# Latent attention: the rotary half of the queries is multiplied out once, its second copy laid by transfers

## The chip, the cores and the metric

The kernel runs on one core of one Trainium2 chip. The metric is the device time of one execution in microseconds (us). A core has TensorE (PE in the profile; its weight loads are the row PEld), VectorE (DVE), ScalarE (ACT), GpSimd (POOL) and SyncE (SP), which here only issues transfers. Each engine works through its own instructions in order and waits at one whose input or buffer is not ready.

## The reference, cut to what matters

Two layers over 256 tokens of width 1024, each with two SwiGLU halves around a token mixer, and a gated embedding behind. The change is in the mixer of the first layer, latent attention with eight heads. A query has 128 plain components and 64 rotary ones; keys and values come from one narrow projection.

```python
c = u @ w_down
c_q, c_kv, k_rope = jnp.split(c, [MLA_Q_LORA, MLA_Q_LORA + MLA_KV_LORA], axis=-1)
q = (rms_norm(c_q, q_norm) @ w_uq).reshape(b, s, MLA_HEADS, MLA_NOPE + MLA_ROPE)
q_nope, q_rope = jnp.split(q, [MLA_NOPE], axis=-1)
q_rope = apply_rope(q_rope, cos[:, :, None, :], sin[:, :, None, :])
k_rope = apply_rope(k_rope, cos, sin)
kv = (rms_norm(c_kv, kv_norm) @ w_ukv).reshape(b, s, MLA_HEADS, MLA_NOPE + MLA_V)
k_nope, v = jnp.split(kv, [MLA_NOPE], axis=-1)
sc = (jnp.einsum('bqhd,bkhd->bhqk', q_nope[:, q0:q1], k_nope[:, :q1])
      + jnp.einsum('bqhr,bkr->bhqk', q_rope[:, q0:q1], k_rope[:, :q1]))
```

The rotation takes the two halves x1, x2 of the 64 components to x1 cos - x2 sin and x2 cos + x1 sin. Scores are masked by chunks of 64 tokens, and softmax and the product with the values follow.

## The kernel before, in words

Activations lie transposed: 128 features on the partitions, 256 tokens along the row. Weights arrive in blocks of 128 x 1024 float32 (`raw`, four buffers). ScalarE rounds a block to a high part (`whi`, line 98), VectorE subtracts to get the low part (`wlo`, line 102: "weight split"), and a product is three: high by high, low by high, high by low (`mm3`, lines 221 to 223). Where both parts of the activations lie side by side, the first and third go as one of 512 columns (lines 236 and 237). `W.pump()` records, at its place in the program, one block's split on VectorE, ScalarE's rounding of up to two blocks ahead, and the fetch of a block four further on; blocks are used in the order of a list, `plan`.

The order on every engine is the order in which the program is written. In `mla` it is: the narrow projection (`pq`, `pkv`, `pr`), its row scale `rb`, the scaled projections and their squares; then `queries(hp, half)` for head pair hp: half 0 are the plain components of two heads (12 products of 256 columns), half 1 the rotary ones (12 products). For the rotation the weight holds the 64 components and, in another 64 columns, the same with their halves swapped. The table `ck` holds the cosine on the first 64 partitions and the signed sine on the other 64, and one multiplication of the 128 rows by `ck` gives what, summed over all 128 partitions against a doubled key (`kr`, made with the matrix `twice`), is the rotated score.

Behind the queries of pair 0 come the keys of all heads (`pk`, 24 products), the values of the first four heads (`values(0, 0)`, `values(1, 0)`), and the row scales: `by_token` (a product `pst`, VectorE's `v`, GpSimd's power `rtok`) and `by_column` (product `pb`, copied by ScalarE to `rb`). `pst` and `pb` share one PSUM buffer. `kT` is `pk` times `rb`, four multiplications on VectorE.

`attention` then runs eleven steps, h = 0 to 10. In step h TensorE does, in this order: fill work, the transposes of head h-3's probabilities (`turn`, `pt`), `project(h, 0)`, the scores of head h-1 (`psc`), `project(h, 1)`, fill work, the value product of head h-3 (`po`). Between them, the maxima `m` and the normalisation of the probabilities `pr` are on VectorE; the exponentials, the copy `ptS` of the transposed probabilities and the copy `os` of a head's result on ScalarE. `project` holds the queries of the pairs to come, and the values of the last four heads (`psv`). Fill work is parts of the output projection over heads that are done, counted per step in `MLA_FILLS` as (step, place): parts. It is done for the first four of eight output blocks; the rest of the products follow behind the last step.

Of the kernel before, what the change touches and what calls it, by code (L numbers as in the profile page):

```python
# [11 lines left out]
F32 = mybir.dt.float32  # L12
# [3 lines left out]
AF = mybir.ActivationFunctionType  # L16
ALU = mybir.AluOpType
AX = mybir.AxisListType

P = 128  # L20
D = 1024
T = 256
# [3 lines left out]
H = 8  # L26
# [3 lines left out]
ROPE = 64  # L30
# [10 lines left out]
GAINS = 80  # L41


MLA_FILLS = {(7, 1): 2, (8, 0): 4, (8, 1): 4, (9, 0): 4, (9, 1): 4, (10, 0): 3, (10, 1): 3}
FOX_FILLS = {(8, 0): 4, (8, 1): 7, (9, 0): 6, (9, 1): 5}

PI_IN = 3.1415925
# [94 lines left out]
def trunk(ctx, tc, xT, xt, pT, pos, freq, bf, ffn_first, ffn_in, ffn_out, w_down, w_uq, w_ukv, mla_o,  # L142
          fox_qk, fox_v, fox_f, fox_o, ple_gate, ple_proj, ple_rows, gain_row, out):
    nc = tc.nc
    const = ctx.enter_context(tc.tile_pool(name="const", bufs=1))
# [3 lines left out]
    work = ctx.enter_context(tc.tile_pool(name="work", bufs=2))  # L149
# [4 lines left out]
    plan = []  # L154
# [11 lines left out]

    plan_ffn(0)
    plan.extend(w_down[c] for c in range(4))
    plan.append(w_uq[0])
    plan.extend(w_ukv[c] for c in range(2))  # L170
    plan.extend(w_uq[c] for c in range(1, H // 2))
    plan.extend(mla_o[d] for d in range(KD))
    plan_ffn(1)
    plan_ple()
# [31 lines left out]
    def bank(name, shape=(P, 2, T)):  # L206
        return psum.tile(list(shape), F32, name=name, tag="mm")

    W = Weights(nc, wp, plan)
# [347 lines left out]
    def mla(norm, nxt):  # L557
# [25 lines left out]
        block(pr, norm.pair)  # L583
        turned = tmp("turned")
        nc.vector.tensor_mul(turned, pr, cr)
        kr = work.tile([P, T], F32, name="kr", bufs=1)
        W.pump()

        kq, v = keys_values()
        kT, qT, qr = kq[:, :8, :], kq[:, 8:16, :], kq[:, 16:24, :]  # L590
        held = []

        def queries(hp, half):
            if half == 0:
                held[:] = W.get()
            ps = bank("ps")
            for s in range(2):
                part(ps[:, s, :], held[0], nq.pair, range(2), at=lambda k: k * 512 + (2 * half + s) * P)
            if half == 0:
                nc.scalar.activation(qT[:, 2 * hp:2 * hp + 2, :], ps, AF.Copy)  # L600
            else:
                W.done(held[0])
                nc.vector.tensor_mul(qr[:, 2 * hp:2 * hp + 2, :], ps,
                                     ck.rearrange("p (o t) -> p o t", o=1).to_broadcast([P, 2, T]))

        queries(0, 0)
        queries(0, 1)
        nkv.by_token()
        W.pump()
        pk = bank("pk", (P, T))  # L610
        nc.tensor.matmul(pk, twice, turned, start=True, stop=True)
        nc.scalar.activation(kr, pk, AF.Copy)
        w, = W.get()
        pk = []
        for hp in range(H // 2):
# [2 lines left out]
                part(ps[:, s, :], w, nkv.pair, range(1), at=lambda k: (2 * hp + s) * P)  # L618
            pk.append(ps)
        W.done(w)  # L620
        w, = W.get()

        def values(t, c):

            ps = bank("psv", (P, 512))
            mm3(ps, [nkv.pair[:, 0, a, t * P:(t + 1) * P] for a in range(2)],
                [a[:, c * 512:(c + 1) * 512] for a in w[1:]], True, True)
            if t == c == 0:
                nkv.by_column()
                for i in range(H // 2):  # L630
                    nc.vector.tensor_mul(kT[:, 2 * i:2 * i + 2, :], pk[i], nkv.rb2)
            nc.scalar.activation(v[:, t, c * 512:(c + 1) * 512], ps, AF.Copy, scale=nkv.rtok[:, t:t + 1])

        values(0, 0)
        nq.by_token()
        W.pump()
        values(1, 0)

        qscale = work.tile([P, 2], F32, name="qscale", bufs=1)
# [1 line left out]
        W.pump()  # L641

        def project(h, half):
            if half == 0 and h < H - 2:
                queries(h // 2 + 1, h % 2)
            elif half and h % 2:
                W.pump()

            if (h, half) == (H - 2, 1):
                values(0, 1)  # L650
            elif (h, half) == (H - 1, 0):
                values(1, 1)
                W.done(w)

        def score(h, dst, diagonal):
            for t in range(2):
                nc.tensor.matmul(dst[t], qT[:, h, t * P:(t + 1) * P], kT[:, h, :(t + 1) * P], start=t == 0, stop=False)
            masked(diagonal, 0)
            for t in range(2):
                nc.tensor.matmul(dst[t], qr[:, h, t * P:(t + 1) * P], kr[:, :(t + 1) * P], start=False, stop=t == 1)  # L660

        attention(project, score, v, qscale, nxt, 3, MLA_FILLS, 4)

# [253 lines left out]
    a = 0  # L917
# [48 lines left out]
    fr = const.tile([P, 1], F32, name="fr")  # L966
    cs = const.tile([P, 2, T], F32, name="cs")
    ck = const.tile([P, T], F32, name="ck")
    twice = const.tile([P, P], F32, name="twice")

    def tables():
        nc.gpsimd.memset(bf_sb, 0.0)
# [93 lines left out]
        for i, a in enumerate(half):  # L1066
            nc.vector.tensor_copy(ck[a, :], cs[a, i, :])
            yield
            for b in half:
                nc.vector.tensor_copy(twice[a, b], ident[a, a])  # L1070
                yield

    n1 = Norm(G_MIX, KD, D)
    ffn(n0, n1, None, first, tables())
# [17 lines left out]
def _cols(w, n):  # L1092

    k, m = w.shape
    return np.ascontiguousarray(w.reshape(k // P, P, m // n, n).transpose(2, 1, 0, 3)).reshape(m // n, P, -1)


def _layout(x, p, positions, ffn_norm, ffn_w_in, ffn_w_out, mix_norm, mla_w_down, mla_q_norm, mla_w_uq,
# [28 lines left out]
    a["w_down"] = _cols(np.concatenate([cq, ckv, kr, ks], axis=1), P)  # L1127

    w = mla_w_uq[0].reshape(256, H // 2, 2, 192)
    nope, rope = w[..., :128], w[..., 128:]  # L1130
    swap = np.concatenate([rope[..., 32:], rope[..., :32]], axis=-1)
    rope = np.concatenate([rope, swap], axis=-1)
    w = np.concatenate([b.reshape(256, H // 2, -1) for b in (nope, rope)], axis=-1)
    a["w_uq"] = _cols(w.reshape(256, -1), 512)
    w = mla_w_ukv[0].reshape(P, H, 2, P)
    a["w_ukv"] = np.ascontiguousarray(w.transpose(2, 0, 1, 3)).reshape(2, P, D)
    a["mla_o"] = _cols(mla_w_o[0], P)
# [42 lines left out]
```

## Time and profile before

| | before |
|---|---|
| median of 3 runs | 1001.46 us (1001.19 to 1002.36) |
| profiled execution, own time | 1001.46 us |
| its span, first to last instruction | 999.7 us |
| granted TensorE clock, mean | 0.998 |
| busy: PE, DVE, ACT, POOL | 988.8, 740.5, 517.6, 423.7 us |
| latent attention, first product to first product of the next stage | 192.00 to 267.12 us of the span |

Timeline rows read: start and duration in us, engine, line, operation, output<-input, shape, count, and in brackets how long the engine stood idle before it and what ended that. TensorE's products overlap: the time that one takes in a stream is the distance between two starts, not its printed duration. Rows of groups end in count, busy time and mean duration.

### The profile page before, as it was taken

How to read it: one execution, taken by the hardware profiler on the slowest of the kernel's cores; microseconds unless marked ns; L12 is line 12 of the kernel's file. 1: busy time of each engine (PE TensorE's matmuls, PEld its weight loads, DVE VectorE, ACT ScalarE, POOL GpSimd, SP SyncE). 2: the span in 40 equal slices, each digit the busy share in tenths (PEclk: the TensorE clock that was granted, in tenths of full speed). 3: DMA queues.
4: the chain of work that ended last, by engine and by line, in shares of the span. 5: the costliest groups of instructions: out<-in, count | busy, mean ns of one | idle time of the engine just before them, and what ended most of it. 6: DMA issues, size and time to landing. Idle time of an engine off the chain costs nothing.

```text
span 999.7 us, 16018 instructions
## 1 busy us (share of the span) xinstructions
PE 988.8 (99%) x5940; PEld 875.1 (88%) x5940; DVE 740.5 (74%) x1051; ACT 517.6 (52%) x825; POOL 423.7 (42%) x348
## 2 busy tenths in 40 slices
PE   9999999999999999999999999999999999999996
PEld 7888888998988888889888888899889888888886
DVE  5777879676768787667778876666777778876674
ACT  7555444456655544555555444546445554544552
POOL 0777730110267775111477673211221577671120
PEclk9999999999999999999999999999999999999999
DMA  8566666651456666665366656666443566666561
GB/s 330 177 209 208 190 181 191 187 169 53 132 182 207 189 190 185 193 196 195 127 198 206 192 182 192 180 194 206 151 142 102 189 202 199 189 179 201 178 210 43
DMA packets 51388, 180.54 MB, mean 181 GB/s; under 512 B 5872, under 2 KB 6000, under 8 KB 51312
## 3 DMA queue, kind: packets, MB, share of 16 engines
q1 hardware_dynamic: 50880, 178.75, 57.3%
q8 instruction: 47, 0.77, 0.3%
q10 hardware_dynamic: 432, 0.79, 0.3%
q14 instruction: 29, 0.24, 0.1%
HBM read 178.46 MB, written 1.05 MB: 180 GB/s over the span
## 4 chain that ended last, share of the span: by engine, by line
PE 91%; DVE 4%; ACT 2%; issue 1%; POOL 0%; DMA 0%; POOLq 0%; SPq 0%; ACTq 0%; DVEq 0%
PE pu L236 16%; PE po L236 16%; PE pg L236 16%; PE po L237 8%; PE pu L237 8%; PE pg L237 8%; PE ps L236 4%; PE ps L237 2%; DVE wlo L102 1%; PE ps L221 1%; PE ps L223 1%; PE ps L222 1%; PE pv L221 1%; PE pv L223 1%; PE pv L222 1%
## 5 line engine op out<-in xcount | busy, mean ns | idle before, releaser
L102 DVE TENSOR_TENSOR wlo<-raw,whi 128x1024 fp32r<-128x1024 f32 (+2 forms) x338 | 416.8, 1241 | 17.8 <-ACT whi L98 17.1
L98 ACT ACTIVATE whi<-raw 128x1024 fp32r<-128x1024 f32 (+2 forms) x338 | 336.4, 1027 | 20.9 <-DMA raw<-in_ffn_in_dram 12.9
L331 POOL TENSOR_TENSOR gu<-two 128x256 f32<-128x256 f32 x176 | 235.5, 1339 | 117.9 <-DVE two L329 108.4
L236 PE MATMUL pg<-u,whi 128*128 128x512 f32 x704 | 251.7, 395 | 0.8 <-ACT whi L98 0.4
L236 PE MATMUL pu<-u,whi 128*128 128x512 f32 x704 | 251.1, 395 | 0.0
L236 PE MATMUL po<-hs,whi 128*128 128x512 f32 x704 | 246.0, 394 | 0.0
L237 PE MATMUL pg<-u,wlo 128*128 128x256 f32 x704 | 198.2, 282 | 0.3 <-DVE wlo L102 0.2
L237 PE MATMUL po<-hs,wlo 128*128 128x256 f32 x704 | 198.1, 281 | 0.0
L237 PE MATMUL pu<-u,wlo 128*128 128x256 f32 x704 | 198.0, 281 | 0.0
L236 PEld LDWEIGHTS pg<-u,whi 128*128 128x128 f32 x704 | 132.2, 188 | 32.1 <-DVE u L280 1.3
L236 PEld LDWEIGHTS pu<-u,whi 128*128 128x128 f32 x704 | 132.2, 188 | 30.3
L236 PEld LDWEIGHTS po<-hs,whi 128*128 128x128 f32 x704 | 132.2, 188 | 30.2
L237 PEld LDWEIGHTS pg<-u,wlo 128*128 128x128 f32 x704 | 132.5, 188 | 0.9 <-DVE wlo L102 0.9
L237 PEld LDWEIGHTS pu<-u,wlo 128*128 128x128 f32 x704 | 132.5, 188 | 0.0
L237 PEld LDWEIGHTS po<-hs,wlo 128*128 128x128 f32 x704 | 132.5, 188 | 0.0
L291 POOL TENSOR_TENSOR acc<-acc,sq 128x256 f32<-128x256 f32 x42 | 46.0, 1094 | 173.7 <-ACT sq L286 173.5
L213 ACT ACTIVATE hs<-hid 128x256 fp32r<-128x256 f32 x88 | 36.8, 418 | 142.1 <-POOL hid L349 140.1
L349 POOL TENSOR_TENSOR hid<-sg,gu 128x256 f32<-128x256 f32 x88 | 105.2, 1196 | 7.0 <-POOL gu L331 0.2
L217 DVE TENSOR_TENSOR hs<-hid,hs 128x256 fp32r<-128x256 f32 x88 | 63.5, 721 | 48.6 <-ACT hs L213 48.6
L329 DVE TENSOR_TENSOR two<-pg,rb 128x512 f32<-128x512 f32 x88 | 60.3, 685 | 46.8 <-PE pg L237 38.9
L275 ACT ACTIVATE u<-state 128x256 fp32r<-128x256 f32 x57 | 29.0, 509 | 125.7 <-DVE state L392 104.3
L343 ACT ACTIVATE sg<-gu 128x256 f32<-128x256 f32 x88 | 36.8, 418 | 78.5 <-POOL gu L331 78.5
(247 smaller groups left out, 1189.2 us busy)
## 6 DMA issues: line engine op xcount, KB each, us to landing
raw<-in_ffn_in_dram SPq DMA_DIRECT2D x172, 512.0 KB, 4.1
raw<-in_ffn_out_dram SPq DMA_DIRECT2D x64, 512.0 KB, 3.6
raw<-in_ffn_out_dram SPq DMA_DIRECT2D x32, 384.0 KB, 3.7
raw<-in_fox_qk_dram SPq DMA_DIRECT2D x16, 512.0 KB, 3.5
raw<-in_mla_o_dram SPq DMA_DIRECT2D x8, 512.0 KB, 4.4
raw<-in_ple_gate_dram SPq DMA_DIRECT2D x8, 512.0 KB, 4.6
raw<-in_fox_o_dram SPq DMA_DIRECT2D x8, 512.0 KB, 3.7
raw<-in_ple_rows_dram SPq DMA_DIRECT2D x8, 512.0 KB, 4.7
```

The costliest lines, as they stand in the source:

```text
L98: self.nc.scalar.activation(self.pairs[i][0][:, c], self.raws[i][:, c], AF.Copy)
L102: self.nc.vector.tensor_sub(lo[:, c], self.raws[i][:, c], hi[:, c].bitcast(F32))
L213: nc.scalar.activation(hi, src, AF.Copy)
L217: nc.vector.tensor_sub(lo, src, hi.bitcast(F32))
L236: nc.tensor.matmul(ps, hi, x[:, k], start=k == 0, stop=False)
L237: nc.tensor.matmul(ps[:, 1, :], lo, x[:, k, 0, :], start=False, stop=k == last)
L275: nc.scalar.activation(self.pair[:, b, 0, c], src[:, c], AF.Copy, scale=g)
L291: nc.gpsimd.tensor_add(new, self.acc, sq)
L329: nc.vector.tensor_mul(two, ps, norm.rb2)
L331: nc.gpsimd.tensor_add(gu[c, i], two[:, 0, :], two[:, 1, :])
L343: nc.scalar.activation(sg, gu.pop((c, 0)), AF.Silu)
L349: nc.gpsimd.tensor_mul(hid[c], gu.pop((c, 0)), gu.pop((c, 1)))
```

## The change

Rotary queries. The weight of a pair now holds the 64 rotary components of each of two heads once, 3 x 128 columns a pair in place of 4 x 128, so half 1 is 6 products of 256 columns. VectorE multiplies the 128 rows by cosine and by sine in one instruction of the old size (`yz`, 2 x 256 columns). Four transfers per pair on SP's queue, each 64 partitions by 256 (64 KB), lay the two parts on the partitions where the score product expects them: for an even head cosine below and sine above, for an odd head the other way. The key is made once (`once` in place of `twice`), and two more transfers lay its halves exchanged as a second form for the odd heads.

Order. Pair 1 is multiplied out before the attention steps, between the keys and the values; pairs 2 and 3 come in steps 0 to 3, so that queries are four heads ahead in place of two. The second product of pair 1 stands between `pb` and `pst`. The values of the last four heads move from the seventh and eighth step (h = 6, 7) to h = 4 and 5. The fills become 26 parts in place of 24, from step 6 on. In `plan` the second query block comes ahead of the second block of keys and values.

```diff
-MLA_FILLS = {(7, 1): 2, (8, 0): 4, (8, 1): 4, (9, 0): 4, (9, 1): 4, (10, 0): 3, (10, 1): 3}
+MLA_FILLS = {(6, 1): 2, (7, 1): 3, (8, 0): 3, (8, 1): 4, (9, 0): 4, (9, 1): 4, (10, 0): 3, (10, 1): 3}
...
-    plan.append(w_uq[0])
-    plan.extend(w_ukv[c] for c in range(2))
-    plan.extend(w_uq[c] for c in range(1, H // 2))
+    plan.extend((w_uq[0], w_ukv[0], w_uq[1], w_ukv[1]))
+    plan.extend(w_uq[c] for c in range(2, H // 2))
...
-        kr = work.tile([P, T], F32, name="kr", bufs=1)
+        kr = work.tile([P, 2, T], F32, name="kr", bufs=1)
...
-            ps = bank("ps")
-            for s in range(2):
-                part(ps[:, s, :], held[0], nq.pair, range(2), at=lambda k: k * 512 + (2 * half + s) * P)
-            if half == 0:
+                ps = bank("ps")
+                for s in range(2):
+                    part(ps[:, s, :], held[0], nq.pair, range(2), at=lambda k: k * 3 * P + s * P)
                 nc.scalar.activation(qT[:, 2 * hp:2 * hp + 2, :], ps, AF.Copy)
-            else:
-                W.done(held[0])
-                nc.vector.tensor_mul(qr[:, 2 * hp:2 * hp + 2, :], ps,
-                                     ck.rearrange("p (o t) -> p o t", o=1).to_broadcast([P, 2, T]))
+                return
+
+            ps = bank("ps", (P, T))
+            part(ps, held[0], nq.pair, range(2), at=lambda k: k * 3 * P + 2 * P)
+            W.done(held[0])
+            yz = work.tile([P, 2, T], F32, name="yz", tag="pair2", bufs=4)
+            nc.vector.tensor_mul(yz, ps.rearrange("p (o t) -> p o t", o=1).to_broadcast([P, 2, T]), cs)
+            for s, (own, other) in enumerate((halves, halves[::-1])):
+                nc.sync.dma_start(qr[own, 2 * hp + s, :], yz[own, 0, :])
+                nc.sync.dma_start(qr[other, 2 * hp + s, :], yz[own, 1, :])
 
         queries(0, 0)
         queries(0, 1)
         nkv.by_token()
+        pk = bank("pk", (P, T))
+        nc.tensor.matmul(pk, once, turned, start=True, stop=True)
+        nc.scalar.activation(kr[:, 0, :], pk, AF.Copy)
+        for own, other in (halves, halves[::-1]):
+            nc.sync.dma_start(kr[other, 1, :], kr[own, 0, :])
         W.pump()
-        pk = bank("pk", (P, T))
-        nc.tensor.matmul(pk, twice, turned, start=True, stop=True)
-        nc.scalar.activation(kr, pk, AF.Copy)
...
         W.done(w)
+        queries(1, 0)
+        nkv.by_column()
+        for i in range(H // 2):
+            nc.vector.tensor_mul(kT[:, 2 * i:2 * i + 2, :], pk[i], nkv.rb2)
+        W.pump()
+        queries(1, 1)
+        nq.by_token()
         w, = W.get()
...
-            if t == c == 0:
-                nkv.by_column()
-                for i in range(H // 2):
-                    nc.vector.tensor_mul(kT[:, 2 * i:2 * i + 2, :], pk[i], nkv.rb2)
...
         values(0, 0)
-        nq.by_token()
-        W.pump()
         values(1, 0)
...
-            if half == 0 and h < H - 2:
-                queries(h // 2 + 1, h % 2)
+            if half == 0 and h < H - 4:
+                queries(h // 2 + 2, h % 2)
             elif half and h % 2:
                 W.pump()
 
-            if (h, half) == (H - 2, 1):
+            if (h, half) == (4, 1):
                 values(0, 1)
-            elif (h, half) == (H - 1, 0):
+            elif (h, half) == (5, 1):
                 values(1, 1)
                 W.done(w)
...
-                nc.tensor.matmul(dst[t], qr[:, h, t * P:(t + 1) * P], kr[:, :(t + 1) * P], start=False, stop=t == 1)
+                nc.tensor.matmul(dst[t], qr[:, h, t * P:(t + 1) * P], kr[:, h % 2, :(t + 1) * P], start=False,
+                                 stop=t == 1)
...
-            for b in half:
-                nc.vector.tensor_copy(twice[a, b], ident[a, a])
-                yield
+            nc.vector.tensor_copy(once[a, :ROPE], ident[a, a])
+            yield
+        for a, b in ((64, 32), (96, 0)):
+            nc.vector.tensor_scalar(once[:, a:a + 32], once[:, b:b + 32], -1.0, None, op0=ALU.mult)
+            yield
...
-    swap = np.concatenate([rope[..., 32:], rope[..., :32]], axis=-1)
-    rope = np.concatenate([rope, swap], axis=-1)
-    w = np.concatenate([b.reshape(256, H // 2, -1) for b in (nope, rope)], axis=-1)
-    a["w_uq"] = _cols(w.reshape(256, -1), 512)
+    w = np.concatenate([b.reshape(256, H // 2, -1) for b in (w[..., :128], w[..., 128:])], axis=-1)
+    a["w_uq"] = _cols(w.reshape(256, -1), 3 * P)
```

Two places where instructions move. The first is VectorE from the scaled keys (`kqv<-ps,rb`, that is `kT`, which waits for `rb`) to the first score maximum (`m`, head 0); `wlo` is a weight split, `kqv<-ps,ck` a rotary product of pair 1, `v` and `qscale` are the two ends of the query row scale, with GpSimd's power `rtok` between them. Before:

```order
L631 TENSOR_TENSOR kqv<-ps,rb 128x512 x4
L308 TENSOR_SCALAR v<-pst 128x2
L102 TENSOR_TENSOR wlo<-raw,whi 128x1024
L640 TENSOR_SCALAR qscale<-rtok 128x2
L102 TENSOR_TENSOR wlo<-raw,whi 128x1024
L603 TENSOR_TENSOR kqv<-ps,ck 128x512
L423 TENSOR_REDUCE m<-psc 128x1
```

And with the change (`yz` are the rotary products of pairs 1 and 2):

```order
L631 TENSOR_TENSOR kqv<-ps,rb 128x512 x4
L102 TENSOR_TENSOR wlo<-raw,whi 128x1024
L606 TENSOR_TENSOR yz<-ps,cs 128x512
L307 TENSOR_SCALAR v<-pst 128x2
L648 TENSOR_SCALAR qscale<-rtok 128x2
L102 TENSOR_TENSOR wlo<-raw,whi 128x1024 x2
L606 TENSOR_TENSOR yz<-ps,cs 128x512
L422 TENSOR_REDUCE m<-psc 128x1
```

Three weight splits and two rotary products stand there in place of two and one, and none of them between `v` and `qscale`.

The second is ScalarE in a step without queries. `pr` are the exponentials of the head whose scores came a step earlier, `os` the result of one head, `ptS` the transposed probabilities of the next. Before, from the `ptS` of step h = 5 to that of h = 6:

```order
L453 ACTIVATE ptS<-pt 128x384
L436 ACTIVATE pr,den<-psc,nm,qscale 128x128
L437 ACTIVATE pr,den<-psc,nm,qscale 128x256
L460 ACTIVATE os<-po 128x256
L453 ACTIVATE ptS<-pt 128x384
```

With the change, from the `ptS` of step h = 4 to that of h = 5:

```order
L452 ACTIVATE ptS<-pt 128x384
L435 ACTIVATE pr,den<-psc,nm,qscale 128x128
L436 ACTIVATE pr,den<-psc,nm,qscale 128x256
L642 ACTIVATE kqv<-psv,rtok 128x512
L459 ACTIVATE os<-po 128x256
L452 ACTIVATE ptS<-pt 128x384
```

The copy of the upper values, `kqv<-psv`, stands between the exponentials and `ptS` there; the second such copy stands at the same place a step later.

More of the change, by code (lines that the diff above doesn't have):

```diff
@@ L591, in mla @@
         held = []
+        halves = slice(0, ROPE), slice(ROPE, P)
         def queries(hp, half):
@@ L968, in trunk @@
     ck = const.tile([P, T], F32, name="ck")
-    twice = const.tile([P, P], F32, name="twice")
+    once = const.tile([P, P], F32, name="once")
     def tables():
@@ L1129, in _layout @@
     w = mla_w_uq[0].reshape(256, H // 2, 2, 192)
-    nope, rope = w[..., :128], w[..., 128:]
-    swap = np.concatenate([rope[..., 32:], rope[..., :32]], axis=-1)
-    rope = np.concatenate([rope, swap], axis=-1)
-    w = np.concatenate([b.reshape(256, H // 2, -1) for b in (nope, rope)], axis=-1)
-    a["w_uq"] = _cols(w.reshape(256, -1), 512)
+    w = np.concatenate([b.reshape(256, H // 2, -1) for b in (w[..., :128], w[..., 128:])], axis=-1)
+    a["w_uq"] = _cols(w.reshape(256, -1), 3 * P)
     w = mla_w_ukv[0].reshape(P, H, 2, P)
```

## The prediction

> **What bounds the kernel now.** I read the page's busy shares and chain first, then busy time in stretches around the edited stage, then the engines' timelines there row by row.
>
> ```profile
> PE 988.8 (99%) x5940; PEld 875.1 (88%) x5940; DVE 740.5 (74%) x1051; ACT 517.6 (52%) x825; POOL 423.7 (42%) x348
> PE 91%; DVE 4%; ACT 2%; issue 1%; POOL 0%; DMA 0%; POOLq 0%; SPq 0%; ACTq 0%; DVEq 0%
> ...
> 212.00:218.00 6.00, 5.53 (x43) 5.06 (x42) 4.61 (x8) 4.01 (x6) 1.60 (x1) 1.00 0.34 115
> 218.00:224.00 6.00, 5.83 (x43) 5.15 (x43) 4.56 (x14) 3.06 (x10) 0.00 (x0) 1.00 0.76 234
> 224.00:236.00 12.00, 12.00 (x84) 10.94 (x82) 7.21 (x27) 5.74 (x19) 0.00 (x0) 1.00 0.02 9
> ```
>
> TensorE (PE) is busy 99% and carries 91% of the chain. In the latent attention (columns of the stretches: length, PE, weight loads, VectorE, ScalarE, GpSimd, clock) it is all but full; the rows below mark three waits of it in brackets, 0.47, 0.17 and 0.30 us. So a matmul removed here is time gained, unless another engine then sets the pace; VectorE (DVE) with 4.61 of 6.00 us is the one near it.
>
> **What is removed.** The 24 query products of the first head pair and what follows them:
>
> ```profile
> 204.36 0.28 PE L221 MATMUL ps<-q,whi 128*128 128x256 f32 x1
> ...
> 207.20 0.28 PE L305 MATMUL pst<-ones,sq 128*128 128x1 f32 x2
> ...
> 207.67 0.70 PE L611 MATMUL pk<-turned,twice 128*128 128x256 f32 x2
> ...
> 211.04 0.39 PE L221 MATMUL psv<-whi,kv 128*128 128x512 f32 x1
> ```
>
> 24 products take 207.20 - 204.36 = 2.84 us, 0.118 each. The rotary half of a pair shrinks from 12 to 6, over four pairs 24 fewer: **-2.84 us**. It comes only where PE does not wait, so I walk the new order with these durations; clock times are those of the trace before.
>
> **First stop: the rotated key.** Product pk needs VectorE's "turned".
>
> ```profile
> 206.06 1.23 DVE L102 TENSOR_TENSOR wlo<-raw,whi 128x1024 fp32r<-128x1024 f32 x1 [0.35 <-ACT whi L98]
> 207.20 0.42 DVE L585 TENSOR_TENSOR turned<-pr,cr 128x256 f32<-128x256 f32 x1
> 207.53 1.22 DVE L102 TENSOR_TENSOR wlo<-raw,whi 128x1024 fp32r<-128x1024 f32 x1
> 208.66 0.68 DVE L603 TENSOR_TENSOR kqv<-ps,ck 128x512 f32<-128x512 f32 x1
> ```
>
> "turned" ends at 207.62 and pk starts at 207.67: already just in time. It stays there: the weight split ahead of it waited 0.35 us for ScalarE, so a shorter split (768 columns) before that one does not help. PE now arrives 6 x 0.118 = 0.71 us earlier and waits: **+0.71** (0 if "turned" moved up with it).
>
> **Second stop: the row scale.** Before, the sum product pst waited for the copy rb, since both use one PSUM buffer:
>
> ```profile
> 211.75 0.61 PE L315 MATMUL pb<-ident,rtok 128*128 128x128 f32 x4
> 212.83 0.61 PE L305 MATMUL pst<-ones,acc 128*128 128x1 f32 x4 [0.47 <-ACT rb L318]
> 213.30 0.48 PE L221 MATMUL psv<-whi,kv 128*128 128x512 f32 x1
> 214.08 0.28 PE L221 MATMUL ps<-q,whi 128*128 128x256 f32 x1
> 212.39 0.38 ACT L318 ACTIVATE rb<-pb 128x256 f32<-128x256 f32 x1 [1.53 <-PE pb L315]
> ```
>
> Now six query products (0.71) lie between pb and pst. pb, at about 0.4 of its own, covers the rest of the 1.08 us from pb to pst: the wait of 0.67 goes, **-0.67**. PE reaches pb at 207.67 + 3.37 + 12 x 0.118 = 212.46, and rb ends 212.46 + 0.64 + 0.38 = 213.48. Then pst at 213.6 (0.47 long), two value blocks (213.30 to 214.08 is one, 0.78) to 215.6, 18 query products (2.13), scores of head 0 at 217.7.
>
> **Third stop: the first softmax.** The place that decides is VectorE's order behind rb, shown with the change. One split more and one rotary product more stand ahead of the first maximum, and nothing is left between v and qscale to fill the time of GpSimd's power.
>
> ```profile
> 212.81 2.49 DVE L631 TENSOR_TENSOR kqv<-ps,rb 128x512 f32<-128x512 f32 x4 [2.26 <-ACT rb L318]
> 215.21 0.15 DVE L308 TENSOR_SCALAR v<-pst 128x2 f32<-128x2 f32 x1
> 217.07 0.17 DVE L640 TENSOR_SCALAR qscale<-rtok 128x2 f32<-128x2 f32 x1 [0.58 <-POOL rtok L310]
> 217.15 1.23 DVE L102 TENSOR_TENSOR wlo<-raw,whi 128x1024 fp32r<-128x1024 f32 x1
> 218.89 0.28 DVE L423 TENSOR_REDUCE m<-psc 128x1 f32<-128x128 f32 x1
> 198.50 0.71 POOL L310 TENSOR_TENSOR rtok<-v,mhalf 128x2 f32<-128x2 f32 x1 [3.90 <-DVE v L308]
> 215.44 1.60 POOL L310 TENSOR_TENSOR rtok<-v,mhalf 128x2 f32<-128x2 f32 x1 [4.33 <-DVE v L308]
> 219.80 0.46 ACT L436 ACTIVATE pr<-psc,nm,qscale 128x128 f32<-128x128 f32 x1 [3.40 <-DVE nm L427]
> 216.95 0.27 PE L657 MATMUL psc<-kqv 128*128 128x128 f32 x1
> 218.19 0.47 PE L221 MATMUL ps<-q,whi 128*128 128x256 f32 x1
> 219.81 0.27 PE L657 MATMUL psc<-kqv 128*128 128x128 f32 x1
> 221.56 0.61 PE L451 MATMUL pt<-ident,pr 128*128 128x128 f32 x3 [0.17 <-DVE pr L444]
> ```
>
> From rb at 213.48: keys 2.40 (212.81 to 215.21) to 215.92; a split 1.13 (207.53 to 208.66) to 217.05; yz at the 0.60 of the old rotary product (same 512 columns out of PSUM; 208.66 to v at 209.26) to 217.65; v to GpSimd 0.23, the power 0.71, since no split runs beside it (1.60 where one did; that end adds 0.9), qscale 0.1: 218.7; two splits 2.27 to 220.97; yz 0.60; the maximum at **221.6**, where it was 218.89. From the maximum to the transposes of head 0 it is 2.67 us before (218.89 to 221.56), with one split inside, as now: transposes at **224.25**. PE is there at 217.7 + 1.24 (scores, 216.95 to 218.19), + 1.62 (12 products behind them, to 219.81), + 1.24 = 221.8. It waits 2.45 us, where it waited 221.56 - (219.81 + 1.24) = 0.51: **+1.94**.
>
> **Fourth stop: the upper values.** They leave the seventh and eighth step (h = 6, 7) for steps h = 4, 5, and so does ScalarE's copy of them. Its order before and after, around a step without queries, is shown with the change. The copy now stands between the exponentials and ptS, the copy of the transposed probabilities, which the next head product needs, in a step without fill work.
>
> ```profile
> 232.51 0.59 PE L458 MATMUL po<-ptS,kqv 128*128 128x256 f32 x2
> 235.62 0.59 PE L458 MATMUL po<-ptS,kqv 128*128 128x256 f32 x2
> 234.90 0.50 ACT L453 ACTIVATE ptS<-pt 128x384 f32<-128x384 f32 x1
> 237.69 0.68 ACT L632 ACTIVATE kqv<-psv,rtok 128x512 f32<-128x512 f32 x1
> 238.26 0.39 ACT L460 ACTIVATE os<-po 128x256 fp32r<-128x256 f32 x1
> 248.97 0.70 PE L458 MATMUL po<-ptS,kqv 128*128 128x256 f32 x2 [0.30 <-ACT ptS L453]
> ```
>
> Before, scores end at 232.51, ptS ends 235.40 (2.89 later), PE wants it at 235.62 (3.11 later): 0.2 us to spare. Steps h = 4, 5 and 6 now have that length. At h = 4 the rotary product (0.60) stands ahead of the maximum, at h = 5 and 6 the copy adds 0.57 (237.69 to 238.26): 0.35 us each, about **+1.0** over the three (0 if the earlier wait leaves ScalarE ahead, 1.7 if none of the 0.2 is to spare). The fills are regrouped (24 to 26 parts of output products ahead of the tail), which leaves their sum as it is; the wait at 248.97 may shrink: **-0.2** (0 to -0.47).
>
> **What is hidden.** Sixteen transfers of yz and two of the key copy join SP's queue, and the splits of w_uq get shorter.
>
> ```profile
> 182.63 0.33 SPq L89 DMA_DIRECT2D raw<-in_w_uq_dram  x1
> raw<-in_mla_o_dram SPq DMA_DIRECT2D x8, 512.0 KB, 4.4
> L102 DVE TENSOR_TENSOR wlo<-raw,whi x338: 944/1215/1769, 15.2 to 975.0; 128x1024 fp32r<-128x1024 f32 x152, 128x768 fp32r<-128x768 f32 x16, 128x1056 fp32r<-128x1056 f32 x1
> ```
>
> No row shows a 64 KB transfer inside the chip; between nothing and the 4.4 us of a 512 KB load, I take the upper end, and 0.33 us per issue. The first pair's yz ends at 209.3, so it has landed by 215.0, and scores of head 0 stand at 217.7. The second's (217.65) has landed by 223.4, and scores of head 2 come after 225. Queued behind the first six transfers is the fetch of a fourth mla_o block, out at 211.3, in at 215.7; ScalarE splits it ahead of the first exponential (222.5). The cover is thus the query products and PE's own wait; a microsecond beyond it would cost a microsecond. The shorter splits (0.944 against 1.215) lie ahead of the ScalarE wait or in VectorE's idle 2.26 us: 0.
>
> **Sum.** -2.84 + 0.71 - 0.67 + 1.94 + 1.0 - 0.2 = -0.06 us. The profiled execution took 1001.46 us (span 999.7 and 1.8 around it), which is also the median. Forecast: **1001.4 us**, no change.
>
> **Rivals.** (a) *The saving arrives*: VectorE is not late at the first softmax, so that wait stays 0.51 and the three after it are nil: -2.84 + 0.71 - 0.67 - 0.2 = -3.0, 998.5 us. For it: VectorE has gaps before (2.26 us ahead of the keys). Against: they lie ahead of rb, and the order puts 8.1 us of VectorE and GpSimd work behind it. (b) *The wait cools TensorE*: the 2.45 us become over 3 (the power at 1.60), and the granted clock drops. The windows above show 1.00 throughout, but no PE wait so long. If PE ran at half speed for the work of one step behind it, 3.11 us by the rows above, that would take 3.1 more: with 0.9 for the power 1001.4 + 4.0 = 1005.4. The Trainium skill, "TensorE: Matmul & The Clock Gate", Part 1, says that an idle window of about 3.4 us halves the clock until some 3.4 us of work have passed; by that rule 2.45 us is short of it, and no run here shows it. (c) *PE waits for the transfers*, at scores of head 2 or 4: head 2's product is covered to 225.4, 2.0 us behind the landing reckoned above; a landing of 8.5 us for 4.4 would cost 2.1: 1003.5. Against it stands that these are an eighth of the bytes of the loads in that row.
>
> **Numbers.** Forecast case 0.82, (a) 0.10, (b) 0.04, (c) 0.04. This kernel's measurement tells about 0.2%, 2.0 us, from no change. The forecast case alone: from -1.3 (no waits at the upper values and none at 248.97) to +1.5 (power at 1.60, those waits at 1.7), 1000.1 to 1003.0. Some of (a) arrives in part, so the range is 999.2 to 1003.0. Faster 0.11, same 0.82, slower 0.07.
>
> **What would show it.** The next stage begins here:
>
> ```profile
> 267.12 0.39 PE L236 MATMUL pg<-u,whi 128*128 128x512 f32 x1
> ```
>
> Right: in the waits of PE, pt from VectorE's pr at about 2.4 us; pk from "turned" 0.7; pst from rb gone; po from ptS some 1 us; 5.5 of 6 us busy or less in the stretch around 222; that first gate product within 1 us of 267.12. Wrong: pt at once, or a wait on a transfer of yz or kr, or a granted clock below 1.00 behind 224.

## The result, and the profile after

| | before | after |
|---|---|---|
| median of 9 runs each | 1001.46 us (1001.11 to 1003.42) | 1004.08 us (1003.02 to 1005.80) |
| profiled execution, own time | 1001.46 us | 1003.26 us |
| its span | 999.7 us | 1001.5 us |
| start of the latent attention (first product of pq) | 192.00 | 191.83 |
| latent attention, to the next stage's first gate product | 75.12 | 74.86 |
| from there to the last product | 724.62 | 726.48 |
| last product to the end | 7.92 | 8.30 |

After to before is 1.0022, 95% interval 1.0011 to 1.0032: the kernel became slower by about 0.2%, 2.6 us in the medians. The forecast was 1001.4 with a range to 1003.0, so it was wrong. The last four rows of the table are parts of the two spans, in us; the parts differ by -0.17, -0.26, +1.86 and +0.38, together 1.8, which is what the profiled executions differ by. The stage that was edited became a little quicker. The 725 us behind it, in which no product was edited, became slower. Executions of one kernel fall in two groups some 1.6 us apart, since GpSimd's first power, at the very start, takes 0.71 us in some traces and 1.54 in others, where PE then waits 1.1 to 1.7 us for it. Five of the nine times before are of the lower group (1001.11 to 1001.46), and five of the nine after are of the upper (1004.08 to 1005.80). The lower groups differ by 1.9 us, so some 0.7 of the 2.6 us is luck, an estimate.

The waits of TensorE (PE) in the attention stage of the changed kernel (columns: us in total, times, longest):

```profile
PE pt L450 <- DVE pr L443: 2.2, 1, 2.2
PE pk L615 <- DVE turned L584: 0.7, 1, 0.7
PE po L457 <- ACT ptS L452: 0.5, 2, 0.3
```

From the timeline of the same kernel, PE, VectorE and GpSimd, and from the groups of transfers the landing time of a rotary part (last number, us):

```profile
207.49 0.70 PE L615 MATMUL pk<-turned,once 128*128 128x256 f32 x2 [0.69 <-DVE turned L584]
224.11 0.61 PE L450 MATMUL pt<-ident,pr 128*128 128x128 f32 x3 [2.18 <-DVE pr L443]
266.69 0.39 PE L235 MATMUL pg<-u,whi 128*128 128x512 f32 x1
...
218.48 0.17 DVE L648 TENSOR_SCALAR qscale<-rtok 128x2 f32<-128x2 f32 x1 [0.80 <-POOL rtok L309]
221.44 0.28 DVE L422 TENSOR_REDUCE m<-psc 128x1 f32<-128x128 f32 x1
217.76 0.69 POOL L309 TENSOR_TENSOR rtok<-v,mhalf 128x2 f32<-128x2 f32 x1 [7.37 <-DVE v L307]
...
kqv<-yz SPq DMA_DIRECT2D x16, 64.0 KB, 2.2
```

And the stretches around the first softmax (length, PE, weight loads, VectorE, ScalarE, GpSimd, clock, share of the DMA engines, GB/s):

```profile
212.00:218.00 6.00, 6.00 (x46) 5.71 (x46) 4.29 (x7) 4.89 (x8) 0.24 (x1) 1.00 0.56 158
218.00:224.00 6.00, 3.93 (x28) 3.21 (x26) 5.37 (x11) 2.21 (x6) 0.45 (x1) 1.00 0.88 268
```

The waits are where the prediction put them. The loss is in rows in which nothing waits. In the dense stages that follow, a block of weights is 16 products. Here are the starts of eight blocks in a row in the kernel before, PE's timeline, only the first product of each block:

```profile
310.20 0.39 PE L236 MATMUL pu<-u,whi 128*128 128x512 f32 x1
...
313.00 0.40 PE L236 MATMUL pg<-u,whi 128*128 128x512 f32 x1
...
315.83 0.40 PE L236 MATMUL pu<-u,whi 128*128 128x512 f32 x1
...
318.64 0.39 PE L236 MATMUL pg<-u,whi 128*128 128x512 f32 x1
...
321.41 0.39 PE L236 MATMUL pu<-u,whi 128*128 128x512 f32 x1
...
324.19 0.39 PE L236 MATMUL pg<-u,whi 128*128 128x512 f32 x1
...
326.96 0.39 PE L236 MATMUL pu<-u,whi 128*128 128x512 f32 x1
...
329.78 0.39 PE L236 MATMUL pg<-u,whi 128*128 128x512 f32 x1
```

and in the changed kernel:

```profile
312.63 0.40 PE L235 MATMUL pg<-u,whi 128*128 128x512 f32 x1
...
315.44 0.39 PE L235 MATMUL pu<-u,whi 128*128 128x512 f32 x1
...
318.25 0.39 PE L235 MATMUL pg<-u,whi 128*128 128x512 f32 x1
...
321.03 0.39 PE L235 MATMUL pu<-u,whi 128*128 128x512 f32 x1
...
323.86 0.39 PE L235 MATMUL pg<-u,whi 128*128 128x512 f32 x1
...
326.65 0.39 PE L235 MATMUL pu<-u,whi 128*128 128x512 f32 x1
...
329.47 0.40 PE L235 MATMUL pg<-u,whi 128*128 128x512 f32 x1
...
332.28 0.40 PE L235 MATMUL pu<-u,whi 128*128 128x512 f32 x1
```

Seven blocks take 329.78 - 310.20 = 19.58 us before and 332.28 - 312.63 = 19.65 after. Before, three blocks (from 318.64) take 2.77 to 2.78, four 2.80 to 2.83; after, only the one from 318.25 is as quick, and the others take 2.79 to 2.83. The pattern returns every seven blocks, and seven is the number of weight buffers (`PAIRS`). With the buffers named 0 to 6 by the place of the high part, the two programs use them in this order: 1 2 3 0 4 6 5 before, 4 3 0 2 6 5 1 after. Buffers 2 and 4 have changed places. This comes from the line of `plan` that puts the second query block ahead of the second block of keys and values: the values' block is held through several steps, so its buffer misses its turn and comes back later in the ring, and now it is another buffer that is held. The median block times of each buffer, worked out from the starts of the products between 300 and 390 us:

| buffer | high part, low part, bytes above a multiple of 256 | before | after |
|---|---|---|---|
| 0 | 128, 0 | 2.773 | 2.774 |
| 4 | 128, 0 | 2.774 | 2.808 |
| 6 | 128, 0 | 2.776 | 2.798 |
| 1 | 0, 128 | 2.806 | 2.808 |
| 5 | 0, 128 | 2.815 | 2.819 |
| 3 | 0, 0 | 2.808 | 2.811 |
| 2 | 128, 128 | 2.828 | 2.829 |

The addresses are those of the built programs and are the same in both; activations (`u`, `hs`) begin 128 above. A dense stage is 66 blocks, three follow, and 3 x 66 x 0.067 / 7 = 1.9 us, which is the 1.86 of the table. In the first dense stage, ahead of the edit, the ring and the times are equal in both kernels.

### The profile page after: what moved, and what is told of

The parts are those of the page before. It is cut to its first block, busy times and chain, and to the rows that moved or that the text cites. A ratio compares the mean times of both kernels' runs of the same rounds, so it can differ in the third digit from the quotient of the medians.

```text
span 1001.5 us, 16002 instructions
## 1 busy us (share of the span) xinstructions
PE 987.8 (99%) x5916; PEld 872.2 (87%) x5916; DVE 740.0 (74%) x1051; ACT 516.0 (52%) x825; POOL 422.3 (42%) x348
## 4 chain that ended last, share of the span: by engine, by line
PE 94%; DVE 3%; ACT 2%; issue 1%; DMA 0%; POOL 0%; POOLq 0%; SPq 0%; DVEq 0%; ACTq 0%
PE pu L235 16%; PE po L235 16%; PE pg L235 16%; PE pg L236 8%; PE po L236 8%; PE pu L236 8%; PE ps L235 5%; PE ps L236 2%; PE ps L222 1%; PE ps L221 1%; PE ps L220 1%; PE pv L220 1%; PE pv L222 1%; PE pv L221 1%; PE po L457 1%
```

## Experiments

Three theories of the loss stood at the start. A: the order of the weight buffers. B: the new stop at the first softmax, or the transfers, leave something slower behind them. C: the second form of the key, 1 KB, moves later tiles. A1 is A with the alignment of the buffers as the reason, A2 with their place in the ring or their neighbour. Because of the two groups, the parts of the span are compared beside the medians: attention stage (first product of pq to first gate product), the rest to the last product, and the end. "Ratio" is to the kernel before on the same chip, with its 95% interval.

| run | median | ratio | attention | rest | end |
|---|---|---|---|---|---|
| before | | | 75.12 | 724.62 | 7.92 |
| after | 1004.08 | 1.0022 (1.0011 to 1.0032) | 74.86 | 726.48 | 8.30 |
| e1, ring put back | 1004.20 | 1.0021 (1.0012 to 1.0029) | 76.07 | 724.71 | 8.29 |
| e8, ring put back, ScalarE spread | 1000.94 | 0.9994 (0.9985 to 1.0003) | 74.16 | 724.65 | 8.29 |
| e2, before with the ring of after | 1004.54 | 1.0019 (1.0011 to 1.0028) | 74.55 | 726.55 | 7.93 |
| e6, after, softmax early | 1001.75 | 0.9997 (0.9988 to 1.0006) | 73.23 | 726.48 | 8.29 |
| e9, e8 with softmax early | 999.19 | 0.9977 (0.9967 to 0.9987) | 72.51 | 724.62 | 8.29 |
| e3, before, one tile | 1001.64 | 0.9993 (0.9984 to 1.0001) | 75.11 | 725.26 | 7.93 |
| e4, after, one tile | 1002.52 | 1.0009 (0.9998 to 1.0019) | 74.86 | 725.24 | 8.32 |
| b1, before, one even tile | 996.91 | 0.9940 (0.9926 to 0.9953) | 75.09 | 721.40 | 7.94 |
| b3, after, one even tile | 997.56 | 0.9947 (0.9934 to 0.9959) | 75.88 | 721.52 | 8.32 |
| b2, b3 with softmax early | 995.27 | 0.9932 (0.9920 to 0.9944) | 73.16 | 721.57 | 8.31 |
| b4, all together | 994.63 | 0.9927 (0.9913 to 0.9941) | 72.42 | 721.47 | 8.31 |

In e1 and e2 the time of an execution is 2.1 to 2.2 us more than its span, in the other runs of the table 1.7 to 1.9; why stays open, and 0.3 us of these two medians lie outside their spans for it.

**The ring alone, in both directions (e2, e1, e8).** e2 is the kernel before with the buffers in the order of the changed one:

```diff
-    plan.append(w_uq[0])
-    plan.extend(w_ukv[c] for c in range(2))
-    plan.extend(w_uq[c] for c in range(1, H // 2))
+    plan.extend((w_uq[0], w_ukv[0], w_uq[1], w_ukv[1]))
+    plan.extend(w_uq[c] for c in range(2, H // 2))
...
-                held[:] = W.get()
+                held[:] = early if hp == 1 else W.get()
...
         W.done(w)
+        early = W.get()
         w, = W.get()
```

> The kernel before with one thing altered: the second query block comes ahead of the second block of keys and values in the plan and is held until it is used, so that the weight buffers follow each other behind the attention as they do with the change. No rotary part, no transfers, no order of TensorE is touched. Theory A: seven blocks take 19.65 us behind the attention, 1003.3 us in all, 1.8 above before. Theories B and C: 1001.5, as before.

The rest took 726.55: an edit that moves no product reproduces what the whole change loses in the rest, with the block times of the table's last column. (The stage became 0.57 shorter. Of the rise of the median to 1004.54, 1.93 is the rest; the two groups and the 0.3 outside the span are in it too.) Theories B and C are out as the main cause, since e2 has neither the stop nor the transfers nor the larger key. e1 is the other direction:

```diff
-    plan.extend((w_uq[0], w_ukv[0], w_uq[1], w_ukv[1]))
+    plan.extend((w_uq[0], w_ukv[0], w_ukv[1], w_uq[1]))
...
         W.done(w)
+        w, = W.get()
         queries(1, 0)
...
         nq.by_token()
-        w, = W.get()
```

> The changed kernel with one thing altered: the second block of keys and values is taken before the second query block, in plan and program, so that the seven weight buffers follow each other behind the attention as they do in the kernel before (2 3 0 4 6 5 1 for the high parts; with the change it was 4 3 0 2 6 5 1). Theory A (a block of 16 products takes 2.77 to 2.83 us according to the buffer it lies in and the one before it; the change swapped two buffers for the rest of the program): seven blocks in a row take 19.58 us again in place of 19.65, the time behind the attention falls by some 1.8 to 2.2 us, 1001.2 us in all, a quarter of a microsecond below before. Theory B (the new stop of TensorE of 2.2 us at the first softmax, or the eighteen new transfers, leaves something slower for the rest): 1004.0, as the change. Theory C (the second key form of 1 KB moves later tiles): 1004.0.

The rest fell to 724.71 as theory A said, but the total did not: 1004.20. Its stage took 1.21 more than in the changed kernel. In its trace, two weight roundings on ScalarE, which had waited for the values' buffer, stand between the values' copy and the copy of `os`, ahead of `ptS`, and a head product waits for them (ScalarE's and PE's timeline):

```profile
237.75 2.00 ACT L98 ACTIVATE whi<-raw 128x1024 fp32r<-128x1024 f32 x2
240.46 0.70 PE L457 MATMUL po<-ptS,kqv 128*128 128x256 f32 x2 [1.76 <-ACT ptS L452]
```

e8 is e1 with these two spread over two steps, each at a place where ScalarE is idle:

```diff
             elif (h, half) == (5, 1):
                 values(1, 1)
+            elif (h, half) == (6, 0):
                 W.done(w)
+                W.live.append(w[0] + 1)
+                W.begin()
+            elif (h, half) == (7, 0):
+                W.live.remove(w[0] + 1)
+                W.begin()
```

> The changed kernel with the values' block taken ahead of the second query block, as before, so that the weight buffers follow each other as in the kernel before; the block's buffer is given back in the seventh step and ScalarE's two roundings that wait for it are spread over two steps, ahead of the exponentials, where ScalarE is idle, since in one place they had held up a head product by 1.8 us. Theory A (the ring is what the change lost): the time from the next stage's first product to the last product is 724.6 us in place of 726.5, no wait of 1.8 takes its place, and the whole is 1.9 to 2.4 under the changed kernel, 1002.0 against 1004.1, or level with the kernel before. If the ring is not the cause: 1004. TensorE's stop of 2.2 us at the first softmax stays, and with it, in some executions, a mean granted clock of 0.996 or less.

It took 1000.94, 3.1 under the changed kernel by the medians and 2.3 by the profiled executions; in the spans 1.83 lies in the rest, and 0.70 in the attention stage, 0.5 of it since the wait for `turned` fell from 0.7 to 0.2. So the ring was the loss, in the changed kernel as well.

**The stop at the first softmax (e6, e9).** e6 is the changed kernel with the sum product `pst` and `v` ahead of the second query pair, and one split two steps later:

```diff
+        nq.by_token()
         queries(1, 0)
...
         queries(1, 1)
-        nq.by_token()
...
-        W.pump()
...
-            elif half and h % 2:
+            elif half and (h % 2 or h == 2):
                 W.pump()
```

> The changed kernel with the first softmax brought forward: the queries' sum product and VectorE's v are taken ahead of the second query pair, so that GpSimd's power runs while VectorE waits for rb, and one weight split moves from ahead of the first maximum to two steps later. The ring of the weight buffers stays as in the changed kernel. If the wait of TensorE at the first transposes (2.2 us) is VectorE's order alone, it falls to 0.3 to 0.8 and the kernel gains 1.4 to 1.9: 1002.4 against 1004.1 for the change. If the wait only moves on to another instruction, nothing is gained, 1004. The blocks behind keep 2.807 on average in both cases.

The first transposes in e6, the two head products there that wait, PE's timeline, and its `v` on VectorE:

```profile
222.51 0.70 PE L450 MATMUL pt<-ident,pr 128*128 128x128 f32 x3 [0.47 <-DVE pr L443]
...
228.64 0.70 PE L457 MATMUL po<-ptS,kqv 128*128 128x256 f32 x2 [0.20 <-ACT ptS L452]
232.27 0.70 PE L457 MATMUL po<-ptS,kqv 128*128 128x256 f32 x2 [0.27 <-ACT ptS L452]
...
211.63 0.16 DVE L307 TENSOR_SCALAR v<-pst 128x2 f32<-128x2 f32 x1 [1.66 <-PE pst L304]
```

The wait fell from 2.18 to 0.47, the stage from 74.86 to 73.23, and nothing took its place: the third stop was VectorE's order, with the price that the prediction gave it. The median fell by more, 2.3 us, but from the upper group to the lower; the lower groups differ by 1.6 (from 1003.02 to 1001.41 for the lowest). What such a stop can cost on top shows in b3's trace. There, after the same idle time, the granted clock was half for 3.41 us (PE's timeline and one stretch of b3; `weven` is a weight tile):

```profile
222.76 0.61 PE L456 MATMUL pt<-ident,pr 128*128 128x128 f32 x3 [2.16 <-DVE pr L449]
223.12 0.36 PE L226 MATMUL ps<-q,weven 128*128 128x256 f32 x1
223.32 0.28 PE L227 MATMUL ps<-q,weven 128*128 128x256 f32 x1
...
223.76 0.42 PE L227 MATMUL ps<-q,weven 128*128 128x256 f32 x1
223.97 0.41 PE L228 MATMUL ps<-q,weven 128*128 128x256 f32 x1
...
227.62 0.49 PE L456 MATMUL pt<-ident,pr 128*128 128x128 f32 x3
...
223.50:227.00 3.50, 3.50 (x15) 2.95 (x15) 1.41 (x5) 1.47 (x5) 0.00 (x0) 0.51 0.77 207
```

Products are 0.21 us apart there in place of 0.12. The step from these transposes to the next ones took 227.62 - 222.76 = 4.86 us, against 3.23 in the profiled execution of the changed kernel, where the clock stayed at 1.00: the price in this step is 1.6 us. 3.41 us at half clock are 0.0017 of the mean clock over the span. Of 48 executions of the five kernels with the stop (after, e1, e4, e8, b3), 18 had a mean clock of 0.996 or less; of 57 executions of the seven without it (e2, e3, e6, e9, b1, b2, b4), none. That the clock fell at this stop is seen in the one trace; in the other executions it is inferred from the mean. e9 is e8 with the early softmax:

> The same with the first softmax brought forward as before. Theory A: 1.4 to 1.9 less again, 1000.4, below the kernel before. If the stop of 2.2 us is what halves TensorE's clock in some executions, none here has a mean clock of 0.996 or less; if the clock falls for another reason, some do, as in the changed kernel.

None of its nine had it, and at 999.19 it is under the kernel before, by 0.23% (0.13 to 0.33).

**What makes a buffer quick or slow (e3, e4, p1 to p4).** e3 and e4 put both parts of a block into one tile; all seven then lie at 128 and 0:

```diff
-        self.pairs[self.begun] = [self.pool.tile([P, n], F32R, name=x, bufs=self.PAIRS) for x in ("whi", "wlo")]
+        both = self.pool.tile([P, 2, WIDE], F32R, name="wpair", bufs=self.PAIRS)
+        self.pairs[self.begun] = [both[:, i, :n] for i in range(2)]
```

> The kernel before with the high and the low part of a weight block in one tile of 2 x 1056 columns, seven of them, in place of seven and seven tiles; the same memory in all, no other change. Every pair of parts then has the alignment of the one buffer that was always quick (high part at 128, low part at 0, in steps of 256 bytes). Theory A1 (the alignment of the two parts sets the pace): every block of 16 products takes 2.774 us in place of 2.797 on average, 0.023 us for each of some 300 blocks, 994.6 us. Theory A2 (it is the buffer's place in the ring or its neighbour, not its address): between 1000 and 1003. Theories B and C say nothing of this and give 1001.5.

> The changed kernel with the same one tile for both parts of a weight block. Theory A1: all blocks at 2.774 us, so the order of the ring no longer matters, and what the change does in the attention stage stands alone: 0.25 below the kernel before with one tile, 994.3 us. Theory B: 1.8 to 2.5 us above the kernel before with one tile. Theory C: the same as B.

Theory A1 failed in its first form: the blocks were alike, but at 2.773 us only in the first dense stage of e3 and at 2.800 everywhere else. The count of PE's products in e3, in a stretch of the first dense stage and in one of the second:

```profile
40.00:130.00 90.00, 90.00 (x521) 79.32 (x520) 71.07 (x89) 47.95 (x71) 68.85 (x53) 1.00 0.67 203
300.00:390.00 90.00, 90.00 (x515) 78.49 (x515) 72.06 (x83) 45.03 (x67) 65.32 (x50) 1.00 0.64 191
```

Same alignment, same clock, 521 products or 515: there is a quick stream and a slow one, and a stage stays in the one that it is in. What did hold is that the order of the ring stopped mattering: e3 and e4 have the same rest, 725.26 and 725.24, where before and after differ by 1.86. To see each alignment by itself, p1 to p4 use six alike tiles per kernel (one execution each, 1005.01 to 1008.13 us; six buffers in place of seven cost something of their own):

```diff
-    RAW, PAIRS = 4, 7
+    RAW, PAIRS = 4, 6
...
-        self.pairs[self.begun] = [self.pool.tile([P, n], F32R, name=x, bufs=self.PAIRS) for x in ("whi", "wlo")]
+        both = self.pool.tile([P, 2304], F32R, name="wpair", bufs=self.PAIRS)
+        self.pairs[self.begun] = [both[:, i:i + n] for i in (32, 1120)]
```

(p1; a spacer keeps what follows in its place. The others begin at other columns, and p4's spacer is 128 bytes longer, which moves all activations.)

> The kernel before with six weight buffers of one tile each, all alike: the high and the low part both begin at a multiple of 256 bytes; activations stay where they were, at 128 above one. It measures what a block of 16 products takes at this alignment; the sixth buffer in place of seven may cost waits elsewhere. Alignment decides: the one buffer of the kernel before that lies so took 2.808 us, so all blocks near 2.81 us. The buffer's neighbour decides: all buffers alike, all near 2.77.

> The same with both parts at 128 above a multiple of 256. Alignment decides: as the slowest buffer of the kernel before, 2.828 us a block. The neighbour decides: near 2.77.

> The same with the high part at a multiple of 256, the low part at 128 above. Alignment decides: as two buffers of the kernel before, 2.806 to 2.816 us a block. The neighbour decides: near 2.77.

> The same with the high part at 128 above, the low part at a multiple of 256 (the alignment of the kernel with one tile for both parts, which took 2.773 or 2.800 us for every block), and all activations moved by 128 bytes to a multiple of 256. If only the weights' alignment matters: 2.773 or 2.800. If it is the weights' alignment against that of the activations: as high part even, low part odd, near 2.82.

| run | high, low, activations (above a multiple of 256) | high and low against activations | us a block, four dense stages |
|---|---|---|---|
| e3, e4 | 128, 0, 128 | same, other | 2.773 or 2.800 |
| p2 | 128, 128, 128 | same, same | 2.827, 2.773, 2.827, 2.773 |
| p1 | 0, 0, 128 | other, other | 2.809 in all |
| p3 | 0, 128, 128 | other, same | 2.816 in all |
| p4 | 128, 0, 0 | other, same | 2.816 in all |

Each matched its alignment, none the neighbour, except that p2 was half of the time in the quick stream, as these four stretches of its dense stages show:

```profile
40.00:130.00 90.00, 90.00 (x511) 78.11 (x510) 70.74 (x86) 47.10 (x69) 67.77 (x53) 1.00 0.68 201
300.00:390.00 90.00, 90.00 (x521) 79.38 (x520) 72.62 (x83) 46.32 (x68) 66.21 (x52) 1.00 0.64 196
510.00:610.00 100.00, 100.00 (x569) 86.76 (x568) 79.73 (x92) 49.47 (x73) 72.79 (x56) 1.00 0.63 193
805.00:900.00 95.00, 95.00 (x549) 83.76 (x550) 77.08 (x90) 48.16 (x72) 70.19 (x54) 1.00 0.64 194
```

p4 against e3 says that it is the alignment against the activations: the same weights' alignment gave 2.816 once the activations were moved by 128 bytes, which is the pace of p3, where all three lie the other way round. The quick stream was seen only where the high part lies like the activations.

**Using it (b1, b3, b2, b4).** In all orders of the ring so far, buffer 0 was quick, and buffer 3, both parts at 0, always stood ahead of it. Buffers 4 and 6 were quick wherever they stood behind 3 and ahead of 2 (both parts at 128), also with 5 and 1 between: in the first dense stage, order 0 6 5 1 4 2 3, buffer 4 took 2.776. In the changed kernel, 2 6 5 1 4 3 0, they stand behind 2 and ahead of 3, and take 2.798 and 2.808. So the exchange of buffers 2 and 4 put two of the three quick blocks into the slow part of the ring. That 3 leads to the quick stream is tried here; that 2 leads to the slow one is read from the orders alone, and p2 shows that blocks of its alignment can run quick too. Six tiles at 128 and 0 and one at 0 and 0 should then lead back to the quick stream once every seven blocks:

```diff
-        self.pairs[self.begun] = [self.pool.tile([P, n], F32R, name=x, bufs=self.PAIRS) for x in ("whi", "wlo")]
+        if self.begun % self.PAIRS:
+            both = self.pool.tile([P, 2112], F32R, name="wpair", bufs=self.PAIRS - 1)
+            starts = 0, 1056
+        else:
+            both = self.pool.tile([P, 2176], F32R, name="weven", bufs=1)
+            starts = 32, 1120
+        self.pairs[self.begun] = [both[:, i:i + n] for i in starts]
```

> The kernel before with the two parts of a block in one tile, where six of the seven tiles have the high part at 128 and the low part at 0 in steps of 256 bytes, and the seventh both at 0 (the table of ones is halved to make room, only its first column is read). Theory A1 as mended: a buffer like the six keeps TensorE in the quick or the slow stream it is in (2.773 or 2.800 us a block, as the kernels with one tile showed in different stages), and a buffer like the seventh ends in the quick one, as it did each time in the kernel before: 2.809 once and 2.774 six times in seven, 2.779 on average in place of 2.797, some 5 us less, 996.5. If the seventh does not lead to the quick stream: 2.801 on average, 1002.5.

> The changed kernel with the same seven tiles. If the ring of the buffers was all that the change lost behind the attention, it is level with the kernel before with these tiles (996.5), within 0.5. If the change costs something else behind the attention: 1.5 to 2.5 above it.

> The changed kernel with these seven tiles and the first softmax brought forward as above: if both gains add up, 1.4 to 1.9 below the changed kernel with the tiles alone, about 994.8, under both kernels.

> The same with the seven tiles, six at 128 and 0 and one at 0 and 0. With these the ring's order should not matter, so what it adds to the kernel with tiles and early softmax is only the first wait on turned, 0.5 us that is gone when the values' block comes first: 994.7, against 995.3.

In b1 a block takes 2.779 on average in all four dense stages, and the same two stretches as above hold more products than in the kernel before (517 and 517):

```profile
40.00:130.00 90.00, 90.00 (x520) 79.26 (x519) 71.49 (x89) 47.38 (x71) 68.96 (x54) 1.00 0.68 202
300.00:390.00 90.00, 90.00 (x521) 79.22 (x520) 72.95 (x84) 45.07 (x67) 65.74 (x51) 1.00 0.65 191
```

b3 has the rest of b1, 721.52 against 721.40: with these tiles the change loses nothing behind the attention. Its stage is 0.79 longer than b1's, with the step of the halved clock in it. b2 and b4 add the early softmax and the ring put back, and b4, at 994.63, is 0.73% under the kernel before.

## Why the prediction was wrong

**The step that failed is "Sum".** It added the stops of one stage, -0.06 us, to the time of the kernel before, and so set every product behind 267.12 at its old price. No term stood for the line of `plan`: the new order was followed for its data (what arrives when), not for its buffers. The runs showed +1.86 us there, with no wait: blocks of 16 products that lie in two of the seven buffers take 2.798 and 2.808 us in place of 2.776 and 2.774, because of the order in which the buffers follow each other (e2, e1, e8). The trace of before had the clue in it: its dense blocks repeat every seven in rows without waits. In the profiled execution every sign of being right that the prediction named was there, the wait for ptS at half its size, and none of the others; all of them lie in the stage, and the loss lies behind it.

**What is removed**, -2.84: right. By the distances between starts the query products take 2.96 less (11.86 before, 8.90 after).

**First stop**, +0.71: the wait is 0.69. **Second stop**, -0.67: the wait for `rb` is gone, 0.47 by its bracket.

**Third stop**, +1.94: right. The maximum came at 221.44 for 221.6, the transposes at 224.11 for 224.25, and the wait in brackets rose from 0.17 to 2.18, by 2.01; the power took 0.69 and qscale waited for it, 0.80. e6 shows that it was VectorE's order.

**Fourth stop**, +1.0: mis-sized. Two waits, 0.46 in all, none at the third place. The prediction's reason for a lower end, that the earlier stop leaves ScalarE ahead, is not it: in e6 that stop is 0.47 and the two waits are the same. What the reckoning of this step had wrong stays open. The late wait is gone, -0.30 for -0.2.

Together these are -2.96 + 0.69 - 0.47 + 2.01 + 0.46 - 0.30 = -0.57. The stage measured 74.86 - 75.12 = -0.26; the other 0.31 is spread over products beside the waits. The forecast was -0.06: as a forecast of the stage it was good to 0.2 us, in part by luck, since the misses of its terms go both ways.

**Hidden**: no wait on a transfer of `yz` or `kr`, rival (c) did not happen; 64 KB landed in 2.2 us, half of the bound of 4.4. **Rival (a)** fell with the third stop.

**Rival (b)** can happen, by the mean clock in 18 of 48 executions with the stop, and from a shorter idle time than the prediction asked for: it set the point at 3 us and the measured stop was 2.2. The price in the step traced was 1.6 us, not 3.1. The clock was no part of the 1.80 between the two profiled executions (1.00 throughout the stage in both), and of the nine executions of the changed kernel one has such a mean clock (0.995, 1005.80 us), so the medians hardly hold it either. The Trainium skill, "TensorE: Matmul & The Clock Gate", Part 1, says that the window of some 3.4 us by which the clock is set is free-running. That agrees: the halved stretch of b3 is 3.41 us long and begins in the middle of a run of products, and equal stops halve the clock in some executions only. Its rule that it takes a whole idle window does not: the 3.41 us ahead of 223.56 held about 2.2 us of idle time and 1.2 of products.

**The end**, +0.38, was in no term either. It stands in all nine kernels with the transfers (8.29 to 8.32) and in none of the eight without (7.83 to 7.94). The last output packet ends 6.36 and 6.37 us behind the start of the last product in the two kernels; SyncE's closing waits end 0.38 later, and the last transfer counts on another semaphore there (110 in place of 108), which is waited for last. That the eighteen transfers shift the numbering is likely, but it was not tried.

## What to carry to other kernels

Where an edit changes how long a buffer of a ring is held, or in which order buffers are taken, write down the ring behind the edit as well as the order in it, and look in the trace for a period of that length in rows without waits. In a kernel that TensorE fills for 700 us, 0.3% of a product's pace (19.65 us for 19.58) was worth more than the change gained in its stage. And a saving that ends in one wait of 2 us on TensorE may cost the clock on top, 1.6 us in b3, in some executions and not in others, so medians need more than one trace.

## What the runs showed of the hardware

TensorE's pace in a steady stream of 512 and 256 columns depends on where the two operands lie modulo 256 bytes (moves of 128 bytes are what was tried): 2.773 to 2.827 us for 16 products, 2%, with no wait in the trace, a granted clock of 1.00, and the engines beside it as busy as ever. Where the high part lies like the activations there are two paces, 2.773 and 2.800 in e3. A stream of such blocks alone keeps its pace through a stage; one block in seven at 0 and 0 brings the quick pace back (b1, 2.779 on average). Why there are two, and what decides at the start of a stage, stays open. The Trainium skill, "SBUF — State Buffer", "SBUF: two separate sides", has TensorE wait for nobody at the memory's engine side. The pace changes with the place all the same: p1, p2 and p3, which differ by 128 bytes in the place of a part, stream at 2.809, at 2.827 or 2.773, and at 2.816. No trace shows what TensorE waits for in it, so the runs do not decide whether that rule is wrong or the reason lies elsewhere.
